# Gated output products of two branches placed between the heads of the attention, four more projections beside branch C

## The chip, the cores and the metric

The kernel runs on one core of one Trainium2 chip. The metric is the device time of one execution in microseconds (us); several executions are timed, and the median is compared. Engines are named as in the profile: PE is TensorE's matmul, PEld its weight load, DVE is VectorE, ACT is ScalarE, POOL is GpSimd, SP is SyncE, whose queue issues all the DMA transfers here. Lower is better.

## What is computed

One inference step of a backbone with two layers on 128 context tokens and 512 latent tokens (640 columns in the kernel), 1024 channels. Each layer normalises and modulates the input to `h`, projects `h` with one wide matrix, feeds three mixers (A grouped-query attention, B multi-head latent attention, C a bidirectional scan), and merges them. Cut from the reference:

```python
def _merge(gates, ya, yb, yc, lp):
    ga, gb, gc = jnp.split(jax.nn.sigmoid(gates), 3, axis=-1)
    mixed = ga * (ya @ lp['w_oa']) + gb * (yb @ lp['w_ob']) + gc * (yc @ lp['w_oc'])
    return mixed @ lp['w_out']

def _latent_mixer(h, lp, row, col, ctx_k, ctx_v, ctx_ckv, ctx_kr, s0_f, s0_b):
    a_q, a_k, a_v, a_z, b_q, b_ckv, b_kr, b_z, c_in, c_z, gates = _split_in(h @ lp['w_in'])
    q, k, v = _a_qkv(a_q, a_k, a_v, lp)
    ...
    ya = _block_attention(...) * jax.nn.silu(a_z)
    ...
    yb = _mla_attend(qb, ckv_all, kr_all, lp) * jax.nn.silu(b_z)
    yc, _, _ = _branch_c(c_in, s0_f, s0_b, lp)
    yc = yc.astype(h.dtype) * jax.nn.silu(c_z)
    return _merge(gates, ya, yb, yc, lp)
```

The products of the change are the three terms of `mixed`: each branch's output (512 channels) times its output matrix, times its sigmoid gate, summed over the branches.

## The kernel before

All of one layer's activations lie with channels on the 128 partitions and the 640 tokens along the free dimension, so that a tile is 128 x 640, worked on in two halves of 320. Each float32 matrix product is made of three matmuls on operands that are split in a high and a low part (`mm3`, L177): ScalarE casts the high part, and VectorE or GpSimd (`self.sub`) subtracts to get the low one. A weight tile is loaded from memory in one or two pieces, cast and subtracted in `load_w1` (L182).

A layer has four stages.

- **Branch C.** Four head pairs `p` go through preparation (`c_prep`, `c_pairs`, `c_inverse`: a long chain on VectorE) and a scan of ten dependent steps (`c_scan`, L700). While pair p is scanned ("period p", L1442), a generator with other work is advanced by `pump` (L201) at a rate worked out from how much it holds: the preparation of pair p+1, and `fillers`: projections of `h` that depend on nothing of the scan. A filler is one projection of 128 channels, `proj_half` twice (L218): 2 x 8 x 3 = 48 matmuls of 320 columns. `PLAN[l]['share']` says how many fillers go before the first scan and into each of the four periods. The list `early` names the projections for attention that are made here and spilled to memory (`spill`, L434, into `cmd[w]`); the 24 gate projections (`gate`, L1249, into `gsp`) follow. Numbers in `early` are projection tiles: 18 to 21 queries of A, 22 and 23 its key and value, 24 to 27 A's output gate paths, 28 to 33 queries of B, 34 to 37 its gate paths, 38 its latent. In period 3 the generator also holds `attention_start` (L1191), with `at` fillers at its six places. Here `c_out` of the pair before runs first, branch C's working memory is closed (`ctx_e.close()`), and A's keys are made by `a_keys` (L1005): `tok` (L888) projects, transposes into the tile `pqt` and copies to `kn` and `vn`.
- **Attention** (L1208). Eight head pairs, four of A and then four of B, each with two heads (`head`, L943): scores `sc` in four blocks, maximum, exponential, transposes `pp`, split, and the product with the values `po`. Between these steps `pump` advances a generator `stream(i)` by `PLAN[l]['rates'][i] / 18`: it prepares the next pair and makes the projections that are not early. `pair_out` (L982) multiplies the pair's output by its gate path and writes it to memory (`ysp`). The generator's rest is drained behind each pair. `PLAN[l]['gates']` can place gate projections here; since all 24 are made beside branch C, the list is empty when attention begins. Fillers share one PSUM bank (tag `f`, `f=1`), and `self.sub` is GpSimd in this stage.
- **Merge** (`merge`, L1258), once for each branch in the order C, A, B. It reads the branch output back (`yr` from `ysp`), splits it, and for each of four weight tiles makes two output tiles `dt`: 2 x 2 x 4 x 3 = 48 matmuls into `pm`, an eviction that multiplies by one plus the gate `gt` (read from `gsp`), and a sum over branches in the tile `mx`, which stays on chip. The last branch splits the sum into `hh` and `hl`. Eight PSUM banks are open here (`f=8`).
- **Out-projection** (`outproj`, L1289), with the next layer's normalisation behind it.

Programs for the engines aren't run in the order in which the functions are called: a planner orders the instructions of each engine by simulated time, first by this order and then by what it takes to be ready, so that later work is issued early when nothing earlier can go.

## Time and profile before

| | us |
|---|---|
| runs | 2320.34, 2323.94, 2329.52 |
| median | 2323.94 |
| profiled execution, its own time | 2325.66 |
| its span, first to last instruction | 2323.9 |
| layer 0: branch C, attention, merge, out-projection | 41 to 774, to 1047, to 1129, to 1195 |
| layer 1: the same | 1195 to 1895, to 2172, to 2254, to 2323.9 |

The stage borders are read from the first scores and the last outputs of attention and from the first matmuls of merge and out-projection; they are good to a microsecond or two, because neighbouring stages overlap. In a table by windows each engine's column is the time in which it ran something, with the number of instructions behind it; PEclk is the mean granted clock of TensorE as a share of full speed.

### The profile page before, as it was taken

The numbers are of one execution on the slowest core, as the hardware profiler recorded it, in microseconds if no ns is written. First come the engines' busy times: TensorE is split into PE (matmuls) and PEld (weight loads), VectorE is DVE, ScalarE is ACT, GpSimd is POOL, SyncE is SP. The second block draws the span as 40 slices with busy tenths as digits, with TensorE's granted clock in tenths as the row PEclk, the third lists the DMA queues.
The fourth block names the chain that finished last, engine by engine and source line by source line (L and its number), as shares of the span: only waits on it lengthen the run. The fifth ranks groups of instructions, "written<-read, shape, count | busy, mean of one in ns | idle before, by whom it ended". The sixth has DMA issues, their size and how long they took to land.

```text
span 2323.9 us, 40367 instructions
## 1 busy us (share of the span) xinstructions
PE 2130.8 (92%) x15380; PEld 2016.8 (87%) x15380; DVE 1589.3 (68%) x3062; ACT 1108.1 (48%) x2462; POOL 690.2 (30%) x761
## 2 busy tenths in 40 slices
PE   8899998999789889989989999999898889999898
PEld 6889998998789778879988999999898777888898
DVE  4676877867845676775648668668677568667673
ACT  4444443544443666662354444434443447667333
POOL 3332527335233221102033133253352332210011
PEclk9999989989899999999999999899797999999899
DMA  6232222222223311126612322222123231110562
GB/s 227 77 102 77 78 73 95 73 93 84 88 91 109 100 38 52 39 77 192 200 53 74 102 73 79 76 94 76 58 74 99 67 101 46 46 55 24 174 191 83
DMA packets 111762, 209.70 MB, mean 90 GB/s; under 512 B 14416, under 2 KB 33488, under 8 KB 111568
## 3 DMA queue, kind: packets, MB, share of 16 engines
q1 hardware_dynamic: 111568, 207.12, 28.1%
q8 instruction: 121, 1.98, 0.4%
q14 instruction: 73, 0.60, 0.1%
HBM read 163.52 MB, written 43.55 MB: 89 GB/s over the span
## 4 chain that ended last, share of the span: by engine, by line
PE 65%; DVE 18%; ACT 7%; DMA 4%; issue 4%; POOL 2%; DVEq 0%; SPq 0%; ACTq 0%; POOLq 0%
PE pcm L225 10%; PE pcm L226 10%; PE pcm L227 10%; PE sc L958 3%; PE sca L767 2%; PE pm L178 2%; PE pm L179 2%; PE pm L180 2%; DVE wlo L175 2%; PE pA L611 2%; PE pp L973 2%; PE px L679 1%; DVE nm L961 1%; PE scb L782 1%; ACT whi L174 1%
## 5 line engine op out<-in xcount | busy, mean ns | idle before, releaser
L225 PE MATMUL pcm<-hh,whi 128*128 128x320 f32 x1952 | 636.0, 326 | 21.7 <-DVE modc L252 6.7
L227 PE MATMUL pcm<-hh,wlo 128*128 128x320 f32 x1952 | 626.1, 321 | 13.7 <-DVE wlo L175 13.6
L226 PE MATMUL pcm<-hl,whi 128*128 128x320 f32 x1952 | 625.9, 321 | 0.0
L225 PEld LDWEIGHTS pcm<-hh,whi 128*128 128x128 f32 x1952 | 381.3, 195 | 29.4 <-DVE modc L252 7.9
L227 PEld LDWEIGHTS pcm<-hh,wlo 128*128 128x128 f32 x1952 | 380.2, 195 | 18.0 <-DVE wlo L175 16.9
L174 ACT CAST whi<-wraw 128x512 fp32r<-128x512 f32 (+1 forms) x356 | 226.6, 666 | 331.3 <-PE pcm L226 122.0
L226 PEld LDWEIGHTS pcm<-hl,whi 128*128 128x128 f32 x1952 | 381.5, 195 | 1.5
L175 DVE TENSOR_TENSOR wlo<-wraw,whi 128x512 fp32r<-128x512 f32 (+1 forms) x262 | 224.4, 871 | 95.1 <-ACT whi L174 91.3
L175 POOL TENSOR_TENSOR wlo<-wraw,whi 128x512 fp32r<-128x512 f32 x94 | 124.1, 1337 | 195.1 <-ACT whi L174 171.1
L778 POOL COPY ubd<-VZ 64x128 f32<-64x128 f32 x160 | 68.0, 425 | 328.1 <-ACT VZ L775 291.1
L164 DVE TENSOR_TENSOR pl<-pp,ph 128x512 fp32r<-128x512 f32 x160 | 108.4, 685 | 47.8 <-ACT ph L163 46.7
L178 PE MATMUL pm<-yh,whi 128*128 128x320 f32 x384 | 121.7, 317 | 7.1 <-DVE OT L995 3.0
L163 ACT CAST ph<-pp 128x512 fp32r<-128x512 f32 x160 | 92.4, 587 | 64.5 <-PE pp L973 53.9
L961 DVE TENSOR_REDUCE nm<-sc 128x1 f32<-128x640 f32 x128 | 104.4, 818 | 25.0 <-PE sc L958 23.6
L179 PE MATMUL pm<-yl,whi 128*128 128x320 f32 x384 | 121.3, 316 | 0.0
L180 PE MATMUL pm<-yh,wlo 128*128 128x320 f32 x384 | 121.0, 315 | 0.0
L963 ACT ACTIVATE P<-sc,nm 128x640 f32<-128x640 f32 x128 | 102.0, 798 | 18.7 <-DVE nm L961 14.4
L973 PE MATMUL pp<-small,P 128*128 128x128 f32 x640 | 102.2, 280 | 7.2 <-ACT P L963 4.3
L973 PEld LDWEIGHTS pp<-small,P 128*128 128x128 f32 x640 | 80.9, 144 | 24.9 <-ACT P L963 5.3
L611 PE MATMUL pA<-L,BK 128*128 128x128 f32 x640 | 90.7, 285 | 11.4 <-ACT AB L616 7.8
L767 PE MATMUL sca<-VZ,L 128*128 128x64 f32 x640 | 93.3, 285 | 7.7 <-DVE VZ L799 7.6
L996 POOL TENSOR_TENSOR OT<-OT,z 128x640 f32<-128x640 f32 x16 | 27.8, 1736 | 239.7 <-DVE OT L995 216.2
(375 smaller groups left out, 5021.6 us busy)
## 6 DMA issues: line engine op xcount, KB each, us to landing
wraw<-in_win SPq DMA_DIRECT2D x156, 256.0 KB, 2.9
wraw<-in_wg SPq DMA_DIRECT2D x96, 256.0 KB, 3.1
wraw<-in_wmod SPq DMA_DIRECT2D x64, 256.0 KB, 2.9
gsp<-gt SPq DMA_DIRECT2D x48, 320.0 KB, 3.1
gt<-gsp SPq DMA_DIRECT2D x48, 320.0 KB, 3.4
wraw<-in_wo SPq DMA_DIRECT2D x24, 512.0 KB, 4.4
cm<-gsl SPq DMA_DIRECT2D x26, 320.0 KB, 2.5
wraw<-in_wmod SPq DMA_DIRECT2D x16, 512.0 KB, 6.5
```

Of the source, the lines that this page charges most:

```text
L174: self.S.copy(out=hi[part], in_=raw)
L175: sub.tensor_tensor(out=lo[part], in0=raw, in1=f32(hi[part]), op=ALU.subtract)
L178: self.PE.matmul(out, lhsT=lh, rhs=rh, start=first, stop=False)
L179: self.PE.matmul(out, lhsT=lh, rhs=rl, start=False, stop=False)
L180: self.PE.matmul(out, lhsT=ll, rhs=rh, start=False, stop=last)
L225: PE.matmul(p[0:m, 0:H], lhsT=wh[:, kt], rhs=self.hh[:, kt, rs], start=(kt == 0), stop=False)
L226: PE.matmul(p[0:m, 0:H], lhsT=wh[:, kt], rhs=self.hl[:, kt, rs], start=False, stop=False)
L227: PE.matmul(p[0:m, 0:H], lhsT=wl[:, kt], rhs=self.hh[:, kt, rs], start=False, stop=(kt == KT - 1))
L611: PE.matmul(pA[:, j * 128:(j + 1) * 128], lhsT=BK[:, u].rearrange("p a s -> p (a s)"), rhs=L1[h][:, u].rearrange("p a s -> p (a s)"), star ...
L767: PE.matmul(a4[:, d, h], lhsT=L1[h][:, uu[d]].rearrange("p a s -> p (a s)"), rhs=VZ[h][:, cc[d], :], start=(h == 0 and d == 0), stop=False ...
L961: V.tensor_reduce(out=nm, in_=sc[:, :, 0:H], axis=AX.XY, op=ALU.max, negate=True)
L973: PE.transpose(p[:, qt * 128:(qt + 1) * 128], Ps[qt][:, t * 128:(t + 1) * 128], ident)
```

## The change

Four things are changed.

1. `merge` is split into `merge_y` (read back and split a branch's output, now one tile `yhl` of 128 x 2 x 4 x 640) and `merge_tile` (one weight tile, 48 matmuls, a generator that yields after every six). Attention calls them inside `stream(i)`: `merge=[0, 1, 1, 2, 0, 1, 1, 2]` tiles in the eight pairs, branch C's four during A's pairs and branch A's four during B's pairs. Only branch B's four remain in the stage behind attention.
2. The sum over branches no longer stays in `mx`: it is written to memory (`mxd`) after branch C, read and written again for branch A, and read for branch B.
3. `early` has four more entries (32, 33, 24, 35), and `share` grows by two fillers in period 2 and two in period 3 of layer 0, by one and three in layer 1. `rates` are set anew; the parameter `gates` goes.
4. To make room, A's key tile `KT` becomes two tiles, and branch B's head keys (`KH`, `KL`) reuse their two buffers.

The diff, cut to its core:

```diff
-    dict(share=[7, 5, 5, 7, 13], fb=[0, 0, 3], at=[3, 2, 1, 0, 2, 1], rate=1.0,
-         early=[38, 29, 19, 20, 21, 26, 37, 23, 28, 18, 30, 31, 34],
-         gates=[1, 0, 0, 0, 0, 1, 1, 0], rates=[8, 8, 22, 30, 21, 16, 25, 13]),
-    dict(share=[8, 6, 7, 7, 9], fb=[0, 0, 1], at=[3, 0, 2, 0, 2, 0], rate=0.8,
-         early=[26, 38, 18, 19, 30, 29, 22, 23, 28, 21, 20, 31, 34],
-         gates=[1, 0, 0, 0, 0, 0, 0, 0], rates=[5, 11, 12, 22, 31, 16, 21, 9]),
+    dict(share=[7, 5, 5, 9, 15], fb=[0, 0, 3], at=[3, 2, 1, 0, 2, 1], rate=1.0,
+         early=[38, 29, 19, 20, 21, 26, 37, 23, 28, 18, 30, 31, 34, 32, 33, 24, 35],
+         merge=[0, 1, 1, 2, 0, 1, 1, 2], rates=[8, 16, 20, 30, 16, 18, 26, 18]),
+    dict(share=[8, 6, 7, 8, 12], fb=[0, 0, 1], at=[3, 0, 2, 0, 2, 0], rate=0.8,
+         early=[26, 38, 18, 19, 30, 29, 22, 23, 28, 21, 20, 31, 34, 32, 33, 24, 35],
+         merge=[0, 1, 1, 2, 0, 1, 1, 2], rates=[8, 16, 20, 30, 16, 18, 26, 18]),
...
-        self.KT = KTt = self.kp.tile([128, 2, 2, 768], F32R, tag="KT", name="KT")
+        self.KT = KTt = [self.kp.tile([128, 2, 768], F32R, tag="KT", name="KT", bufs=2) for _ in range(2)]
...
-        KH = ap.tile([128, 768], F32R, tag="KH", name="KH", bufs=2)
-        KL = ap.tile([128, 768], F32R, tag="KL", name="KL", bufs=2)
+        KHL = self.kp.tile([128, 2, 768], F32R, tag="KT", name="KHL", bufs=2)
+        KH, KL = KHL[:, 0], KHL[:, 1]
...
+            yw = {}
+            def units(i):
+                br = 2 if i < 4 else 0
+                if br not in yw:
+                    yw[br] = self.merge_y(l, br, self.ap, "yhl", self.ap)
+                for _ in range(self.plan.merge[i]):
+                    yield from self.merge_tile(l, br, todo[br].pop(0), yw[br], wp, gp, ps)
...
                 yield from self.gate_z(es[i], l, W_AZ if i < 4 else W_BZ, wp, ps)
-                yield from units(n // 2)
                 if 3 <= i < 7:
                     self.b_pair2(l, e, ps)
                     self.b_head(l, e, 0, ps)
-                yield from units(n - n // 2 if i < 7 else len(gates))
+                yield from units(i)
                 return e
...
+    def merge_y(self, l, b, pool, tag, yp):
+        yhl = pool.tile([128, 2, 4, T], F32R, tag=tag, name="yhl", bufs=1)
         for k in range(4):
-            yr = gp.tile([128, T], F32, tag="yr", name="yr")
-            nc.sync.dma_start(out=yr, in_=self.ysp[b][k])
-            self.split(yh[k // 2][:, k % 2], yl[k // 2][:, k % 2], yr, 0.5)
+            yr = yp.tile([128, T], F32, tag="yr", name="yr", bufs=self.nyr)
+            self.nc.sync.dma_start(out=yr, in_=self.ysp[b][k])
+            self.split(yhl[:, 0, k], yhl[:, 1, k], yr, 0.5)
+        return yhl
+
+    def merge_tile(self, l, b, dp, yhl, wp, gp, ps):
+        nc, V, G = self.nc, self.V, self.G
+        oh, ol = self.load_w1(wp, self.I["wo"][l, b, dp])
+        for j in range(2):
+            dt = dp * 2 + j
+            c0 = j * 128
+            gt = gp.tile([128, T], F32, tag="gt", name="gt")
+            nc.sync.dma_start(out=gt, in_=self.gsp[b][dt])
+            if b != 2:
+                m = gp.tile([128, T], F32, tag="m", name="m", bufs=self.nm)
+                nc.sync.dma_start(out=m, in_=self.mxd[dt])
+            for half in range(2):
+                hs = slice(half * H, half * H + H)
+                pm = ps.tile([128, 512], F32, tag="f", name="pm")
+                for k in range(4):
+                    self.mm3(pm[:, 0:H], oh[:, k, c0:c0 + 128], ol[:, k, c0:c0 + 128], yhl[:, 0, k, hs],
+                             yhl[:, 1, k, hs], k == 0, k == 3)
+                    if k % 2:
+                        yield
+                V.scalar_tensor_tensor(out=gt[:, hs], in0=gt[:, hs], scalar=1.0, in1=pm[:, 0:H], op0=ALU.add, op1=ALU.mult)
+            if b != 2:
+                (G if b == 0 else V).tensor_tensor(out=gt, in0=m, in1=gt, op=ALU.add)
+            if b != 1:
+                nc.sync.dma_start(out=self.mxd[dt], in_=gt)
+            else:
+                self.split(self.hh[:, dt], self.hl[:, dt], gt, 0.5)
...
-                gp = pool(ctx, f"gp3{l}", 2)
+                self.nyr, self.nm = 2, 3
+                gp = pool(ctx, f"gp3{l}", 3)
...
-                    self.merge(l, 2, wp, gp, yp, mx, ps)
-                    self.merge(l, 0, wp, gp, yp2, mx, ps)
...
-                self.merge(l, 1, wp, gp, yp, mx, ps)
+                yhl = self.merge_y(l, 1, yp, "yhl", gp)
+                for dp in range(4):
+                    self.play(self.merge_tile(l, 1, dp, yhl, wp, gp, ps))
```

## Rows read from the trace of the kernel before

**Rows 1.** The page: busy us (share of the span) xinstructions of each engine.
```profile
PE 2130.8 (92%) x15380; PEld 2016.8 (87%) x15380; DVE 1589.3 (68%) x3062; ACT 1108.1 (48%) x2462; POOL 690.2 (30%) x761
```

**Rows 2.** Busy time by windows, five stages (columns: window and length, engines, clock, DMA).
```profile
core 0: us, PE busy (x) PEld busy (x) DVE busy (x) ACT busy (x) POOL busy (x), PEclk, DMA share, GB/s
41.00:774.00 733.00, 669.47 (x5230) 645.25 (x5228) 509.12 (x1021) 330.69 (x756) 282.01 (x321) 0.94 0.28 88
774.00:1047.00 273.00, 248.03 (x1524) 215.78 (x1525) 202.12 (x377) 181.10 (x413) 46.98 (x39) 0.95 0.16 52
1047.00:1129.00 82.00, 82.00 (x557) 82.00 (x557) 52.47 (x75) 22.15 (x26) 14.60 (x9) 0.99 0.64 196
...
1195.00:1895.00 700.00, 642.18 (x4864) 624.25 (x4863) 491.58 (x983) 302.50 (x696) 243.57 (x297) 0.92 0.25 79
1895.00:2172.00 277.00, 251.40 (x1565) 222.22 (x1566) 199.37 (x378) 184.11 (x420) 49.63 (x40) 0.95 0.17 54
```

**Rows 3.** Groups of instructions in layer 0's merge window: xcount, busy us, mean ns, idle before.
```profile
L178 PE MATMUL pm<-yh,whi 128*128 128x320 f32 x186 | 57.8, 311 | 0.0
...
L175 DVE TENSOR_TENSOR wlo<-wraw,whi 128x1024 fp32r<-128x1024 f32 x13 | 18.3, 1407 | 2.1 <-ACT whi L174 2.0
...
L1280 DVE SCALAR_TENSOR_TENSOR gt<-gt,pm 128x320 f32<-128x320 f32 x28 | 12.9, 483 | 12.8 <-DMA gt<-gsp 7.9 <-PE pm L179 2.9 <-PE pm L180 1.9
...
L1285 DVE TENSOR_TENSOR gt<-mx,gt 128x640 f32<-128x640 f32 x6 | 4.9, 821 | 0.1
...
L166 ACT ACTIVATE yh<-yr 128x640 fp32r<-128x640 f32 x6 | 4.3, 737 | 15.3 <-DMA yr<-ysp 10.2 <-PE pm L179 5.1
L167 DVE SCALAR_TENSOR_TENSOR hl<-gt,hh 128x640 fp32r<-128x640 f32 x5 | 4.1, 820 | 0.8 <-ACT hh L166 0.8
```

**Rows 4.** Timeline where layer 0's attention ends: start us, us, engine, line, tiles, idle before.
```profile
1045.22 2.01 POOL L996 TENSOR_TENSOR OT<-OT,z 128x640 f32<-128x640 f32 x1 [15.79 <-DVE OT L995]
1045.23 0.61 PE L178 MATMUL pm<-yh,whi 128*128 128x320 f32 x1 [1.49 <-DVE OT L995]
```

**Rows 5.** DMA issues of the page: xcount, KB each, median us from issue to landing.
```profile
yr<-ysp SPq DMA_DIRECT2D x24, 320.0 KB, 3.3
...
ysp<-OT SPq DMA_DIRECT2D x16, 320.0 KB, 2.3
```

**Rows 6.** Timeline of PE and of ACT around the end of period 2, layer 0.
```profile
613.93 0.38 PE L895 MATMUL pqt<-small,qcm 128*128 128x128 f32 x2
...
657.96 0.74 ACT L896 COPY kn<-pqt 128x512 f32<-128x512 f32 x2
```

**Rows 7.** Busy time by windows: ends of branch C, layer 0 and then layer 1.
```profile
612.00:655.00 43.00, 29.10 (x281) 26.85 (x279) 29.36 (x68) 14.71 (x42) 12.81 (x24) 0.68 0.19 63
...
700.00:733.00 33.00, 31.77 (x233) 30.95 (x232) 14.61 (x37) 11.67 (x32) 7.74 (x10) 0.95 0.31 99
733.00:774.00 41.00, 35.31 (x262) 33.67 (x262) 21.89 (x53) 14.87 (x32) 16.95 (x12) 0.97 0.50 154
...
1775.00:1815.00 40.00, 31.42 (x246) 28.70 (x244) 21.45 (x57) 8.66 (x29) 13.89 (x28) 0.70 0.09 31
...
1835.00:1865.00 30.00, 25.20 (x165) 23.43 (x162) 12.51 (x33) 15.53 (x39) 5.90 (x10) 0.89 0.34 108
1865.00:1895.00 30.00, 23.64 (x152) 22.26 (x151) 20.70 (x38) 9.38 (x22) 12.36 (x8) 0.89 0.30 94
```

**Rows 8.** Busy time by windows: the densest head pair of each layer's attention.
```profile
986.00:1020.00 34.00, 32.35 (x220) 29.48 (x220) 25.74 (x43) 24.71 (x57) 2.28 (x2) 1.00 0.25 82
...
2103.00:2136.00 33.00, 32.74 (x227) 30.22 (x226) 24.18 (x42) 23.21 (x53) 2.28 (x2) 1.00 0.03 11
```

**Rows 9.** Single tiles and lines: xcount, duration ns min/median/max, first and last start.
```profile
L175 POOL TENSOR_TENSOR wlo<-wraw,whi x13: 1263/1269/1296, 773.0 to 951.6; 128x512 fp32r<-128x512 f32 x13
...
L1283 POOL TENSOR_TENSOR mx<-mx,gt x16: 1562/1577/2628, 1077.4 to 2226.8; 128x640 f32<-128x640 f32 x16
...
L164 DVE TENSOR_TENSOR pl<-pp,ph x160: 671/684/693, 784.3 to 2163.2; 128x512 fp32r<-128x512 f32 x160
```

**Rows 10.** Waits of PE in layer 0's attention: us in total, times, longest us.
```profile
PE pq L1065 <- DVE z L424: 2.6, 1, 2.6
```

More of the change, by code (lines that the diff above doesn't have):

```diff
@@ L155, in __init__ @@
         self.bsp = [dr.tile([128, T], F32, tag=f"bsp{p}", name=f"bsp{p}") for p in range(4)]
+        self.mxd = [dr.tile([128, T], F32, tag=f"mxd{k}", name=f"mxd{k}") for k in range(KT)]
         self.zsp = [dr.tile([128, T], F32, tag=f"zsp{p}", name=f"zsp{p}") for p in range(4)]
@@ L1039, in a_keys @@
                     for c in range(2):
-                        S.copy(out=KTt[c * 64:c * 64 + 64, g, j, t0 * 128:(t0 + n) * 128],
+                        S.copy(out=KTt[g][c * 64:c * 64 + 64, j, t0 * 128:(t0 + n) * 128],
                                in_=p[g * 64:g * 64 + 64, 0:n * 128])
@@ L1066, in a_pair2 @@
             self.split_q(QT, slice(t0 * 128, (t0 + n) * 128), p[:, 0:n * 128])
-        e.keys = [[(QT[:, h], self.KT[:, g, 0]), (QT[:, h], self.KT[:, g, 1])] for h in range(2)]
+        e.keys = [[(QT[:, h], self.KT[g][:, 0]), (QT[:, h], self.KT[g][:, 1])] for h in range(2)]
         e.VS = lambda h: self.VSa[:, :, g, :]
@@ L1206, in attention_start, with attention @@
         return [e, (yield from self.a_pair(l, 1, wp, gp, ps))]
-    def attention(self, l, es, wp, gp, ps, gates):
+    def attention(self, l, es, wp, gp, ps):
         with self.tc.tile_pool(name=f"ap{l}", bufs=1, reuse_waits="tile") as self.ap:
-            def units(n):
-                for _ in range(min(n, len(gates))):
-                    yield from gates.pop(0)
+            yw = {}
[5 more added lines that the diff above has]
+                    yield from self.merge_tile(l, br, todo[br].pop(0), yw[br], wp, gp, ps)
             def stream(i):
-                n, e = self.plan.gates[i], None
+                e = None
                 if i < 3:
@@ L1408, in run @@
                     self.early.add((l, w))
-                ng = sum(plan.share) - len(units)
-                units += [self.gate(l, *g, wp, st, ps) for g in gates[:ng]]
-                del gates[:ng]
+                units += [self.gate(l, *g, wp, st, ps) for g in gates]
+                assert len(units) == sum(plan.share)
                 mods = [(l, ct) for ct in range(2 * KT, 3 * KT)]
@@ L1481, in run @@
                 ps = P(f"psB{l}", f=1, pt=2, po=1, S=2)
-                self.attention(l, x, wp, st, ps, [self.gate(l, *g, wp, st, ps) for g in gates])
+                self.nyr, self.nm = 1, 1
+                self.attention(l, x, wp, st, ps)
                 self.sub = self.V
@@ L1488, in run @@
                 self.pieces, self.nraw, self.nw = 1, 2, 2
-                gp = pool(ctx, f"gp3{l}", 2)
+                self.nyr, self.nm = 2, 3
+                gp = pool(ctx, f"gp3{l}", 3)
                 mp = pool(ctx, f"mx{l}", 1, side="right")
-                mx = mp.tile([128, KT, T], F32, tag="mx", name="mx")
                 wop = pool(ctx, f"wop{l}", 1, side="right")
-                yp = pool(ctx, f"yw{l}", 4)
-                with ExitStack() as ctx2:
-                    yp2 = pool(ctx2, f"yv{l}", 4)
-                    self.merge(l, 2, wp, gp, yp, mx, ps)
-                    self.merge(l, 0, wp, gp, yp2, mx, ps)
+                yp = pool(ctx, f"yw{l}", 1)
                 op = pool(ctx, f"op{l}", 2)
-                self.merge(l, 1, wp, gp, yp, mx, ps)
-                xs = mp.tile([128, KT, T], F32, tag="mx", name="xs")
+                yhl = self.merge_y(l, 1, yp, "yhl", gp)
+                for dp in range(4):
+                    self.play(self.merge_tile(l, 1, dp, yhl, wp, gp, ps))
+                xs = mp.tile([128, KT, T], F32, tag="xs", name="xs")
                 self.outproj(l, xs, wop, wp, op, ps)
```

26 lines of the change are left out of this document (1 added, 25 removed).

## The prediction

> **What bounds the kernel now.** I read the page first: TensorE (PE) is called busy 92% of the span, VectorE (DVE) 68% [rows 1]. So TensorE's issue looks like the bound, and the question is where it still has holes. The stage table [rows 2] answers it. Each layer has four stages: branch C (733.0 and 700.0 us), attention (273.0 and 277.0), the gated output products, here "merge" (82.0; layer 1's is alike and stands for it), and the out-projection. The column to read is PEld, the weight loads, one ahead of each matmul: 100% of the merge window, 88% and 89% of the two branch C windows, 79% and 80% of the attentions. The merge issued 557 matmuls in 82.00 us, 0.147 us each; this is the price of a dense matmul here. A "unit" (a projection tile or a merge tile) is 48 matmuls, 7.07 us. The merge has 12 units a layer and no hole; attention has 57.2 and 54.8 us without a weight load, branch C 87.8 and 75.8. The change carries units from the full stage into the two that have holes.
>
> The Trainium skill, Trace Analysis, Identifying the Most-Contended Engine, calls matmul busy share a bad metric and names weight-load share instead. The trace agrees: in the merge matmuls overlap so far that means of 311 ns [rows 3] pass at 0.147 us each. Read by matmul busy, attention would have 25.0 and 25.6 us of room for 28.3 us of work; with half of it usable attention would cost 31 us and not the 14 below, and the sum would be 2282.
>
> **The change part by part.**
>
> Merge. Eight of the 12 units a layer leave (branches C and A), four stay (branch B). Before, TensorE ran merge matmuls without a hole from 1045.23 [rows 4] to the end of the merge window at 1129, 84 us. After, 192 matmuls are 28.3 us, but branch B needs the last head pair's output, which has just been made. That chain was hidden under branches C and A: GpSimd's product 2.0 us [rows 4], write 2.3, read back 3.3 [rows 5], cast 0.74 and subtraction 0.82 [rows 3], 9.2 us. Its cover now is the first three of four k steps of eight PSUM banks, 72 matmuls or 10.6 us, just enough. Behind it VectorE is late next: 16 evictions of 0.483, 8 additions of 0.82, 8 subtractions of 0.82, and weight subtractions of 1.41 for two more output tiles and the first two out-projection tiles [rows 3], 7.7 + 6.6 + 6.6 + 5.6 = 26.5 us. I take 9.2 + 26.5 = 36 us, so the stage gives back 48 a layer, 96 in all. Bounds: TensorE alone, 28.3 (gain 56); transfers alone, about 9.6 MB (gates and partial sums 5.2, weights 2.1 and 1.0, outputs 1.3) at the 196 GB/s of the window [rows 2], 49 us (gain 35). I stay nearer to VectorE's figure because its instructions are all in the rows, while 196 GB/s is what was asked for, not a limit.
>
> Branch C. Four more projections a layer: two in period 2 and two in period 3 of layer 0, one and three in layer 1. Each also issues two weight loads and one write-out on SyncE's queue, which is mostly idle there; their casts, subtractions and evictions go to ScalarE and VectorE, 45% and 69% busy in that stage [rows 2]. Period 2 ends in a hole. The transposes of a projected tile (pqt) were issued at 613.93, long before their turn, and their copies out to kn ran only at 657.96 [rows 6]: the memory of kn is that of branch C, free only when the normalised scan output of pair 2 is out. Until then the transposes hold the PSUM banks of the projections and no projection runs. In 612 to 655 weight loads ran 26.85 of 43.00 us at a granted clock of 0.68, a mix of the levels 1.2 and 2.4 GHz; in layer 1, 1775 to 1815, 28.70 of 40.00 at 0.70 [rows 7]. Units that come earlier in the order push later ones into the hole: 14.1 us into 16.2, 7.1 into 11.3. I put them at nothing. If the cover is gone they cost 21.2; if the clock stays at the lower level there, two units want twice 14.1 and don't fit. Period 3's units have less: 14.1 us against 2.1 + 7.3 of room in layer 0, 21.2 against 6.6 + 7.7 in layer 1 [rows 7]. I let half of the room be usable: 14.1 - 4.7 = 9.4 and 21.2 - 7.2 = 14.0, so branch C costs 23 in both layers. Ends: all room usable, 12; none anywhere, 57.
>
> Attention. Four projections leave (28.3 us), eight merge tiles come (56.6), net 28.3 a layer. Weight loads and added pitch make 215.8 + 28.3 = 244.1 and 250.5 us. The densest pairs before had 29.48 of 34.00 (87%) and 30.22 of 33.00 (92%) [rows 8]. At 87% the stages take 281 and 288, at 92% 265 and 272. I take 87%, nearer to a stage in which most pairs have work, less 1.8 a layer for a dozen branch C matmuls that already ran inside the last pair: +6 and +9, about 14 with the rounding. Ends: -8 a layer, and +28.3 with nothing hidden. The other engines have room: VectorE is at 74%, ScalarE 66%, GpSimd 17% [rows 2]. Per layer GpSimd gains 8 weight subtractions net of 1.27 and 8 additions of 1.58 [rows 9], 22.8 us on an engine with 226 idle; VectorE gains 32 evictions of 0.483 and 8 subtractions of 0.82, 22 us on 71 idle, less what four projections took. SyncE's queue gets 64 transfers (16 weight loads, 16 gates, 24 of partial sums, 8 branch outputs) and four read-backs for eight weight loads that go; the stage moves 52 GB/s against 196 in the merge, so I put them at nothing too. The split key buffer (KT in two halves that later hold branch B's keys) adds a wait of b_head on branch A's scores; these run early in a pair, and I put it at nothing; the first branch B keys late by one pair's scores would be a few us once a layer.
>
> Sum: -96 + 23 + 14 = -59. The profiled execution took 2325.66 us, 1.7 over the median of 2323.94 and inside the runs shown; 59 off the median is 2265.
>
> **The rivals.**
>
> Better: the holes take nearly all. Branch C costs 12, attention gains 8 a layer: 2324 - 96 + 12 - 16 = 2224. For it: the merge shows that TensorE can be at 100%. Against: no attention pair was above 92%.
>
> Late merge tiles: the planner leaves the last two tiles of branch A in pair 7 to the drain behind the heads, where nothing hides them: 14.1 a layer, 2293. For it: tile sums of pairs 0 and 4 are empty and pair 7 has two. Against: the planner ran merge matmuls inside pair 7 before.
>
> Slower, no room: each moved unit costs its 7.07 us in the new place, 113 in all, against 96: 2341. This is the case that the change only shifts work; it decides when less than 15% of the moved work (17 of 113) falls into holes. Against it: the holes of [rows 7].
>
> Slower, one bank: in attention fillers share one PSUM bank. A projection hands it over twice, a merge tile four times: 16 handovers a layer before, 8 + 32 = 40 after. One handover shows as a TensorE wait: 2.6 us for z's eviction [rows 10]. If each of the 24 new ones stalled so, 62 a layer would replace attention's 14: 2265 - 14 + 123 = 2374. It turns the change into a loss above (59 + 14) / 48 = 1.5 us each. Against: one of about 16 handovers shows so.
>
> GpSimd against VectorE: if GpSimd's added 22.8 us a layer blocked VectorE and VectorE bound, 46 us would go: 2311. Against: GpSimd's subtraction in attention took 1263 to 1296 ns and VectorE's 671 to 693 over all 160 [rows 9], no stretch; its additions reached 2628 at most. The Trainium skill, SBUF — State Buffer, SBUF: two separate sides, describes such a rule: one of the two holds a shared port pair for its whole instruction while the other waits. By it this rival would come true.
>
> **How the numbers follow.** Forecast 0.62 (2265, by the bounds some 2240 to 2300), better 0.13, late tiles 0.10, port 0.05, no room 0.06, one bank 0.04. The range 2228 to 2314 leaves out the two slower cases and half of the better one, under 0.2. About 0.5%, 12 us, is what a measurement can tell from no change. Faster: 0.62 less a tail of 0.03, plus 0.13 and 0.10, is 0.82; within 0.5%: 0.05 and the tail, 0.08; slower 0.10.
>
> **What the profile of the changed kernel would show.** The merge window from the last attention matmul to the first out-projection one: 36 us (28 to 48) with VectorE near full in it, else my chain is wrong. Attention 273 and 277 become about 279 and 286 with weight loads at 87%. Branch C grows by about 9 and 14, the holes at the ends of period 2 get shorter by two units and one, and their granted clock rises from 0.68 and 0.70. If attention grows by more than 28, with waits of TensorE for evictions of pm, the one-bank rival is right; a stretched GpSimd or VectorE row says the port; a tail of pm matmuls behind the last PV product of pair 7 says late tiles. The prediction is wrong if the holes don't shrink, or if the first merge matmul of branch B comes more than 10 us after the last of attention.

## The result, and the profile after

The changed kernel took 2395.84 us (median of four runs, 2393.60 to 2397.68), the kernel before 2322.52 (four runs): 1.031 times, 95% interval 1.0286 to 1.0334. It is slower by 73 us where 59 less were forecast. Its profiled execution took 2393.60 us with a span of 2391.8, 67.9 more than that of before. Line numbers of the changed kernel are higher by one to some fifteen.

The page's busy times, as in [rows 1]: TensorE has the same 15380 matmuls, and smaller shares of a longer span.

```profile
PE 2149.5 (90%) x15380; PEld 2034.3 (85%) x15380; DVE 1577.8 (66%) x3062; ACT 1112.1 (46%) x2478; POOL 703.0 (29%) x777
```

The stages by windows, attention and merge of layer 0, then of layer 1; they answer to [rows 2].

```profile
core 0: us, PE busy (x) PEld busy (x) DVE busy (x) ACT busy (x) POOL busy (x), PEclk, DMA share, GB/s
805.00:1117.00 312.00, 269.59 (x1647) 239.17 (x1646) 209.66 (x397) 180.88 (x409) 63.90 (x52) 0.92 0.25 80
1117.00:1173.00 56.00, 40.64 (x237) 39.18 (x238) 23.65 (x35) 13.34 (x16) 4.70 (x4) 0.79 0.65 224
1946.00:2265.00 319.00, 274.37 (x1679) 243.58 (x1679) 211.10 (x408) 185.98 (x420) 66.13 (x54) 0.92 0.26 85
2265.00:2322.00 57.00, 43.21 (x265) 41.64 (x266) 25.04 (x39) 13.56 (x16) 6.43 (x5) 0.88 0.67 225
```

Layer 1's attention of the kernel before begins with its first scores at 1892, 3 us ahead of the border in [rows 2], and ends at 2171. Cut like the rows above it is

```profile
1892.00:2171.00 279.00, 252.44 (x1576) 223.00 (x1576) 201.77 (x385) 184.14 (x420) 50.60 (x41) 0.95 0.18 55
```

Read the second column of busy times, PEld, against the length. The attentions had 57.2 and 56.0 us without a weight load; they have 72.8 and 75.4 now. They were given 28.3 us of work each, grew by 39 and 40, and their holes grew. The merge stage was one block at 100%; 30% and 27% of it are empty now, at a granted clock of 0.79 and 0.88.

For the comparison of kernels I cut every trace at four events of a layer: branch C begins with the first `plo` matmul and ends with the first context scores (`scc`), attention ends with the last product of `OT` and `z` on GpSimd, merge with the first `pout` matmul. Layer 0 / layer 1:

| kernel | its us | before beside it | branch C | attention | merge |
|---|---|---|---|---|---|
| before | 2323 | | 733 / 696 | 273 / 279 | 82 / 83 |
| changed | 2396 | 2323 | 763 / 710 | 312 / 319 | 56 / 57 |
| e1 projections only | 2340 | 2326 | 763 / 714 | 255 / 263 | 83 / 81 |
| e2 branch C's tiles only | 2367 | 2326 | 760 / 706 | 297 / 306 | 60 / 60 |
| e3 other bank | 2334 | 2326 | 762 / 706 | 314 / 320 | 29 / 28 |
| e5 last pair free | 2369 | 2326 | 762 / 705 | 312 / 336 | 42 / 36 |
| e6 bank alone | 2360 | 2320 | 733 / 696 | 291 / 300 | 81 / 82 |
| e7 merges alone, bank | 2324 | 2320 | 729 / 695 | 328 / 340 | 28 / 29 |
| e8 C's tiles in B's pairs | 2364 | 2320 | 738 / 697 | 311 / 323 | 61 / 58 |
| e9 third gate buffer | 2377 | 2320 | 765 / 706 | 306 / 317 | 51 / 57 |
| e10 merges alone | 2406 | 2330 | 734 / 694 | 342 / 350 | 53 / 57 |
| e11 bank in pairs 4 to 6 | 2358 | 2330 | 765 / 709 | 322 / 329 | 27 / 28 |
| e12 merges alone, the same | 2343 | 2330 | 737 / 699 | 331 / 337 | 29 / 35 |
| e13 spread tiles | 2343 | 2330 | 767 / 707 | 310 / 329 | 27 / 28 |
| e14 period 2's units alone | 2324 | 2317 | 741 / 707 | 266 / 265 | 83 / 83 |
| e15 merges, period 2, bank | 2351 | 2317 | 746 / 702 | 329 / 339 | 27 / 29 |
| e16 the same, spread | 2373 | 2317 | 738 / 702 | 340 / 362 | 29 / 28 |
| e17 with gate buffer | 2352 | 2317 | 735 / 702 | 330 / 353 | 29 / 29 |
| e18 merges, bank, buffer | 2326 | 2321 | 733 / 692 | 331 / 337 | 28 / 28 |
| e19 change, bank, buffer | 2330 | 2321 | 762 / 707 | 314 / 320 | 28 / 27 |

e1 to e17 are single executions beside one of before; in the last comparison 19 executions of before lay between 2314.50 and 2336.64, so a difference of less than some 15 us between single times says little, and the stages say more. Changed less before by stage: branch C +30.6 and +13.3, attention +39.2 and +39.9, merge -25.7 and -26.6, out-projection -2.9 and +0.1: 67.9, all of the difference.

Two places of layer 0 stand for the loss. First the tail. The timeline behind the heads, and a wait of SyncE's queue in it:

```profile
1120.82 0.49 DVE L1295 SCALAR_TENSOR_TENSOR gt<-gt,pm 128x320 f32<-128x320 f32 x1 [3.84 <-DMA gt<-gsp]
1132.11 0.49 DVE L1295 SCALAR_TENSOR_TENSOR gt<-gt,pm 128x320 f32<-128x320 f32 x1 [3.66 <-PE pm L181]
1134.29 0.32 SPq L1299 DMA_DIRECT2D mxd<-gt  x1
1136.44 0.80 SPq L1271 DMA_DIRECT2D yr<-ysp  x2
1137.29 0.42 SPq L174 DMA_DIRECT2D wraw<-in_wo  x1
1142.79 1.04 ACT L175 CAST whi<-wraw 128x1024 fp32r<-128x1024 f32 x1 [1.88 <-DMA wraw<-in_wo]
1143.89 0.64 PE L179 MATMUL pm<-yhl,whi 128*128 128x320 f32 x1 [11.82 <-ACT whi L175]
```

```profile
SPq L1271 <- DMA mxd<-gt: 1.8, 1, 1.8
```

The heads end at 1117, but branch A's last tile still runs, a bank at a time, until its last partial sum goes out at 1134.29. Only when that write has landed are branch B's output, weights and gates asked for (1136.44, 1137.29), and TensorE stands idle for 11.82 us. In the kernel before, the read-backs for the merge began at 1026.62, during pair 7; the first were branch C's, which had long been there. Then the first merge matmuls of branch B run slowly. Windows of that stretch:

```profile
1131.00:1144.00 13.00, 1.18 (x6) 0.78 (x4) 2.26 (x4) 2.52 (x3) 1.53 (x1) 0.50 0.55 193
1144.00:1150.00 6.00, 6.00 (x33) 6.00 (x34) 2.71 (x3) 1.90 (x3) 0.00 (x0) 0.77 1.04 410
1156.00:1173.00 17.00, 17.00 (x118) 17.00 (x117) 14.77 (x23) 8.15 (x10) 0.00 (x0) 1.00 0.73 241
```

Matmul by matmul that is 6.00 us / 33 = 0.18 us at a clock of 0.77, between the levels of 1.2 and 2.4 GHz, against 17.00 / 118 = 0.144 at 1.00.

Second, a border of pairs. TensorE where pair 4 gives over to pair 5:

```profile
992.92 0.63 PE L1151 MATMUL pqr<-small,qr 128*64 128x128 f32 x4 [0.41 <-DVE gt L1295]
994.14 0.44 PE L921 MATMUL scc<-KHL,QT 128*128 128x128 f32 x2 [0.60 <-DVE QT L168]
998.58 0.33 PE L921 MATMUL scc<-KB,QR 96*128 96x128 f32 x1 [2.61 <-DVE QR L1158]
1002.15 0.40 PE L1151 MATMUL pqr<-small,qr 128*64 128x128 f32 x1 [2.38 <-DVE QR L1158]
```

The next pair's query transposes (`pqr`) got the f bank at 992.92, released by the eviction (`gt`) of a merge tile. Pair 5's scores had begun at 994.14 with the part that needs `KHL` and `QT` alone; the rest waited for `QR`, which is made from `pqr`. The bank is not all of this wait. ScalarE, which takes `pqr` out, first cast a projection's weights and a row of a branch output for the merge tiles (`yhl`), and came to `QR` at 996.10:

```profile
994.02 1.14 ACT L175 CAST whi<-wraw 128x512 fp32r<-128x512 f32 x2
995.06 0.73 ACT L167 ACTIVATE yhl<-yr 128x640 fp32r<-128x640 f32 x1
996.10 0.59 ACT L1156 ACTIVATE QR<-pqr 32x512 fp32r<-32x512 f32 x1
```

Pair 4 has no merge tile by plan. The ones that ran there are the two of pair 3, a pair late, in both layers. The merge matmuls alone, in changed's pair 4 and then in pair 3 of e3, the kernel with these transposes in another bank (below), where they ran in time:

```profile
950.00:999.00 49.00, 15.81 (x96) 14.26 (x96) 3.90 (x8) 0.91 0.30 99
913.00:971.00 58.00, 15.84 (x96) 14.21 (x96) 4.38 (x9) 0.93 0.38 121
```

PE's waits in layer 0's attention, in us, times, longest; neither `scc` nor `pqr` had more than 0.9 from QR in the kernel before:

```profile
PE sc L959 <- ACT P L964: 6.4, 7, 2.0
PE scc L921 <- DVE QR L1158: 4.6, 2, 2.6
PE pqr L1151 <- DVE QR L1158: 2.6, 2, 2.4
PE pqr L1151 <- DVE z L425: 1.9, 1, 1.9
PE pm L179 <- DVE gt L1295: 1.6, 3, 0.8
```

### The profile page after: what moved, and what is told of

Read it like the earlier page. It is cut to its first block, busy times and chain, and to the rows that moved or that the text cites. A ratio compares the mean times of both kernels' runs of the same rounds, so it can differ in the third digit from the quotient of the medians.

```text
span 2391.8 us, 40580 instructions
## 1 busy us (share of the span) xinstructions
PE 2149.5 (90%) x15380; PEld 2034.3 (85%) x15380; DVE 1577.8 (66%) x3062; ACT 1112.1 (46%) x2478; POOL 703.0 (29%) x777
## 4 chain that ended last, share of the span: by engine, by line
PE 35%; DVE 8%; ACT 4%; DMA 3%; issue 2%; POOL 1%; DVEq 0%; SPq 0%; ACTq 0%; POOLq 0%
PE pcm L226 5%; PE pcm L227 5%; PE pcm L228 5%; PE pm L179 2%; PE pm L180 2%; PE pm L181 2%; PE pout L179 1%; PE sc L959 1%; PE pout L181 1%; PE pout L180 1%; PE sca L768 1%; PE pA L612 1%; PE pp L974 1%; DVE L L550 1%; DVE BK L548 1%
## 5 line engine op out<-in xcount | busy, mean ns | idle before, releaser
L176 DVE TENSOR_TENSOR wlo<-wraw,whi 128x512 fp32r<-128x512 f32 (+1 forms) x262 | 201.9, 790 | 97.4 <-ACT whi L175 94.1
L176 POOL TENSOR_TENSOR wlo<-wraw,whi 128x512 fp32r<-128x512 f32 x110 | 145.5, 1337 | 263.2 <-ACT whi L175 232.2
L179 PE MATMUL pm<-yhl,whi 128*128 128x320 f32 x384 | 125.8, 331 | 36.1 <-ACT whi L175 22.4
L964 ACT ACTIVATE P<-sc,nm 128x640 f32<-128x640 f32 x128 | 102.0, 798 | 41.8 <-DVE nm L962 36.0
L180 PE MATMUL pm<-yhl,whi 128*128 128x320 f32 x384 | 121.2, 317 | 0.0
L181 PE MATMUL pm<-yhl,wlo 128*128 128x320 f32 x384 | 118.4, 316 | 0.0
L962 DVE TENSOR_REDUCE nm<-sc 128x1 f32<-128x640 f32 x128 | 104.3, 819 | 20.5 <-PE sc L959 19.4
L179 PEld LDWEIGHTS pm<-yhl,whi 128*128 128x128 f32 x384 | 74.8, 195 | 41.0 <-ACT whi L175 23.0
L768 PEld LDWEIGHTS sca<-VZ,L 128*128 128x128 f32 x640 | 91.7, 211 | 18.5 <-DVE VZ L800 17.7
```

The costliest lines, as they stand in the source:

```text
L176: sub.tensor_tensor(out=lo[part], in0=raw, in1=f32(hi[part]), op=ALU.subtract)
L179: self.PE.matmul(out, lhsT=lh, rhs=rh, start=first, stop=False)
L180: self.PE.matmul(out, lhsT=lh, rhs=rl, start=False, stop=False)
L181: self.PE.matmul(out, lhsT=ll, rhs=rh, start=False, stop=last)
L768: PE.matmul(a4[:, d, h], lhsT=L1[h][:, uu[d]].rearrange("p a s -> p (a s)"), rhs=VZ[h][:, cc[d], :], start=(h == 0 and d == 0), stop=False ...
L962: V.tensor_reduce(out=nm, in_=sc[:, :, 0:H], axis=AX.XY, op=ALU.max, negate=True)
```

## The experiments

None of the kernels leaves out a part of the computation. "Changed" is the changed kernel.

**The two parts apart.** The kernel before with the projections only, then with the merge tiles only:

```diff
 # e1, on before
-    dict(share=[7, 5, 5, 7, 13], ... early=[..., 31, 34],
+    dict(share=[7, 5, 5, 9, 15], ... early=[..., 31, 34, 32, 33, 24, 35],
 # e10, on changed
-    dict(share=[7, 5, 5, 9, 15], ... early=[..., 31, 34, 32, 33, 24, 35], ... rates=[8, 16, 20, 30, 16, 18, 26, 18]
+    dict(share=[7, 5, 5, 7, 13], ... early=[..., 31, 34], ... rates=[8, 16, 20, 36, 16, 26, 26, 18]
```

> The kernel before with the four more early projections and their shares alone; all merge tiles stay behind attention. Attention loses 4 projections (28.3 us of matmuls) a layer, the merge stage stays. Theory 1 (the loss sits between branch B's heads and in the tail, branch C costs what the changed kernel shows, 31 + 13): branch C grows by about 44 in both layers, attention gives back 10 to 25 a layer, so 2322 + 44 - 35 = about 2331, between 2315 and 2350. Theory 2 (a unit costs its 7.07 us wherever it stands): 2322, no change. Theory 3 (the four projections are the main cause, attention had room for them): 2355 or more.

> The changed kernel with before's projections beside branch C (no four early ones); banks and merge tiles as changed. Theory 1 (the two parts of the change add): the changed kernel less what the projections alone cost, 2392 - 14 = 2378 (2365 to 2390), branch C as in before. Theory 2 (the loss comes from the two parts together, branch C's growth shifting the attention): within 12 of before, 2311 to 2335.

e1: branch C +30.5 and +17.6, attention -17.9 and -15.8. Moving 28.3 us a layer cost more in branch C than attention gave back; 14 us slower, inside the range of its theory 1. e10 took 2406, 76 above its before, and misses both its theories; the parts don't add (14 + 76 is more than 73): with the merge tiles in it, attention gains more from losing four projections (342 to 312, 350 to 319) than it did without them (273 to 255, 279 to 263).

> The kernel before with only period 2's early projections (two in layer 0, one in layer 1); period 3's four and the merge tiles stay as before. Theory 1 (period 2's units run in its hole and cost nothing, and attention loses 0.6 to 1.0 of their 7.07 us): branch C as before within 4 a layer, attention -9 to -14 in layer 0 and -4 to -7 in layer 1, 2302 to 2313 beside a before of 2326. Theory 2 (each unit costs its 7.07 us and a stall in branch C as period 3's did): branch C +14 to +25 and +7 to +12, 2326 to 2345.

e14 is e1 with `share=[7, 5, 5, 9, 13]` and `[8, 6, 7, 8, 9]`, so only period 2's. Branch C +8.4 and +10.2, attention -7.3 and -14.6; the time, 7 above its before, is within what single executions tell, and the 13 to 24 us less of its theory 1 didn't come. The units were not free, and attention gave back about what branch C took.

**The bank.** The next pair's transposes and values off the f bank, in changed (e3) and in the kernel before (e6); e11 does it in pairs 4 to 6 alone, e12 the same without the early projections:

```diff
-            p = ps.tile([128, 512], F32, tag="f", name="pqr")
+            p = ps.tile([128, 512], F32, tag=self.prep, name="pqr")
 # the same for pvb, and (e3, e6, e7, e8, e18, e19) for pq
 # self.prep is "pt" in attention; in e11 and e12 only from pair 4 on, in e15 to e17 from pair 3 on
```

> The changed kernel, but the next pair's query transposes and value products (pq, pqr, pvb) take the two PSUM banks of the head's transposes (tag pt) in attention and no longer the one bank that merge tiles use. Theory 1 (merge tiles hold the one bank, the next pair's preparation comes late, its scores start cold): pairs 4 to 6 fall by 20 us a layer or more from 141, the kernel to about 2350. Theory 2 (no bank matters, the work is just too much): 2396 within 10, or slower by what the heads' transposes lose.

> The kernel before, with one edit: in attention the next pair's transposes (pq, pqr) and value products (pvb) take the two pt banks and no longer the one f bank; no merge tile moves. Theory 1 (the bank matters only where merge tiles hold it long): the time of before, 2326, within 6. Theory 2 (the one f bank already limited attention before the change): each attention falls by some 8 to 10 us, 2306 to 2310.

> The changed kernel with the next pair's transposes and value products (pqr, pvb) on the pt banks only while pairs 4 to 6 run; pairs 0 to 3 keep the f bank. Theory 1 (the bank edit costs in pairs 0 to 3, +17 to +22 a layer where it stood alone, and gains in pairs 4 to 7 and the tail): pairs 0 to 3 as in the changed kernel (146, 149), pairs 4 to 7 near 150, merge 28, 2295 to 2310. Theory 2 (the gain needs the tiles to end early in pair 3, which only the wide edit does): pairs 4 to 7 stay at 160 or more, merge above 45, 2340 to 2385.

> As the run before it, with before's projections beside branch C. Theory 1: branch C as in before, attention about 15 to 20 a layer longer than there, 2285 to 2305. Theory 2 (attention has no room for four more units): attention above 330, 2325 or more.

e3 took 2334, 62 less than changed. But the gain isn't in attention's length (314 and 320): it is the merge stage, 29 and 28 against 56 and 57. The tiles were no longer held up, none was left behind the heads, and branch B's tiles began in time. Its theory 1 named the bank, but looked for the gain in pairs 4 to 6, which fell by 14 and 7 us and not by 20 a layer. Attention by windows, both layers of e3 and then of e6:

```profile
803.00:1117.00 314.00, 280.82 (x1706) 247.97 (x1707) 214.68 (x406) 183.72 (x413) 70.24 (x55) 0.93 0.32 103
1915.00:2235.00 320.00, 286.29 (x1759) 253.51 (x1759) 218.15 (x417) 188.44 (x424) 73.05 (x57) 0.94 0.33 109
774.00:1064.00 290.00, 257.38 (x1528) 222.08 (x1529) 203.88 (x377) 181.19 (x412) 45.43 (x39) 0.93 0.15 49
1906.00:2206.00 300.00, 264.69 (x1575) 229.08 (x1575) 201.61 (x385) 184.39 (x420) 48.82 (x41) 0.93 0.16 51
```

e3's holes are 66.0 and 66.5 us where changed had 72.8 and 75.4, with the late tiles inside. Cut by pairs, at the last product of `OT` and `z`, e3's pairs 4 to 7 are 20.5 and 18.2 us shorter than changed's, its pairs 0 to 3 are 21.6 and 19.1 longer; 14.1 us of that are the two tiles that came back from pair 4. e6, the same edit without tiles, cost 40 us against its before, nearly all of it in attention (+17.5 and +21.2); both theories miss. All of that lies in pairs 0 to 3 (+16.8 and +21.6; pairs 4 to 7 +0.7 and -0.3), and its holes are 67.9 and 70.9. Why A's pairs pay so much for it stays open. e11 has the tail of its theory 1 (27 and 28) and the long B pairs of its theory 2 (178 and 180). e12 with 2343 and attentions of 331 and 337 is its theory 2: no room for four more units.

**Merge tiles elsewhere.** e2 has branch C's tiles between heads and branch A's behind attention, e5 no tile in the last pair, e8 branch C's in B's pairs and branch A's behind attention, with before's projections and the other bank, e13 is e11 with one tile in each A pair:

```diff
-merge=[0, 1, 1, 2, 0, 1, 1, 2]
+merge=[0, 1, 1, 2, 0, 0, 0, 0]   # e2
+merge=[1, 1, 1, 1, 0, 2, 2, 0]   # e5
+merge=[0, 0, 0, 0, 1, 1, 1, 1]   # e8, branch C's
+merge=[1, 1, 1, 1, 0, 1, 1, 2]   # e13
```

> The changed kernel, but branch A's four merge tiles stand behind attention again, ahead of branch B's; branch C's stay between the heads of A's pairs. Theory 1 (branch A's tiles in branch B's pairs and the tail behind them cost more than they save): pairs 4 to 7 come back to 130 us a layer or less from 167 and 169, the wait of 11.8 us ahead of branch B's first matmul goes, the merge stage is 28 us of matmuls longer, and the kernel takes about 2396 - 2 x 37 - 2 x 20 + 2 x 28 = 2338, between 2310 and 2355. Theory 2 (a unit costs 7.07 us anywhere): four units out of attention and four into the merge cancel, 2396 within 10.

> The changed kernel with merge tiles at other places: branch C's one in each of pairs 0 to 3, branch A's two in pairs 5 and 6, none in pair 7. Tail part of theory 1 (branch B's loads can't start before the last branch A tile has freed its memory, and pair 7's tiles run behind the heads): branch B's loads start before attention ends, the 11.8 us wait goes, and the stretch from the last head output to the out-projection falls from 56 to about 40 a layer; attention itself stays within 10 us: about 2396 - 32 = 2364, between 2345 and 2385. Theory 2: the same units, 2396 within 10.

> Before's projections, the next pair's transposes and values on the pt banks, and only branch C's four merge tiles between heads, one in each of the pairs 4 to 7; branch A's tiles stand behind attention with branch B's. Theory 1 (a merge tile costs its 7.07 us of TensorE wherever it stands): merge gives back 28 a layer, attention takes 28 a layer, 2326 within 8. Theory 2 (the pairs of branch B have holes that one tile each can fill, and the loss of the changed kernel came from crowding two into one pair): attention +15 a layer, 2300 (2290 to 2312).

> The changed kernel with the narrow bank edit of pairs 4 to 6 and branch C's tiles one to each of the pairs 0 to 3 (two stood in pair 3). Theory 1 (two tiles in pair 3 lag into pair 4): pairs 4 and 5 shorter by 5 to 10 a layer than with the tiles as changed, 10 to 20 us less in all. Theory 2 (a tile costs 7 us wherever it stands): within 6 of the kernel with the narrow edit alone.

e2 against e1: four tiles (28.3 us) made attention 41.8 and 42.9 longer and merge only 23 and 21 shorter. So branch C's tiles alone lose, before any tail; e2 has changed's rates and buffers too, so it is not the tiles by themselves. e5's stages behind the heads are 42 and 36: the tail falls by 14 and 21, but layer 1's attention takes 16 back. e8 was worse than either theory. e13 is 14 below e11, as its theory 1 had it, but inside what single executions tell; e16 further on is 23 above e15 by the same move (rates set along with it in both). No rule came of where the tiles stand.

**The gate rows.** A buffer more for `gt` in attention (e9):

```diff
-            gt = gp.tile([128, T], F32, tag="gt", name="gt")
+            gt = (self.ap if j and self.nm == 1 else gp).tile([128, T], F32, tag="yr" if j and self.nm == 1 else "gt", name="gt", bufs=1 if j and self.nm == 1 else None)
```

> The changed kernel with a third buffer for the gate rows of the merge tiles in attention (the second row tile of each merge tile takes a buffer of its own), all else as changed. Theory 1 (the single bank and TensorE's full order set the pace of the merge tiles): the changed kernel's 2392 within 8. Theory 2 (the evictions of pm wait for gate rows, which wait for the write-out of the row tile before, and so hold the bank): pairs 3 to 7 and the tail lose 10 to 15 a layer, 2362 to 2372, and the wait of the last evictions for gt is gone.

In attention (`nm` is 1) the second row tile of each merge tile takes a buffer of its own. e9 took 2377, between its theories. VectorE's waits in changed from 1105 to 1135, and then in e9 from 1080 to 1135:

```profile
DVE gt L1295 <- PE pm L181: 11.9, 6, 3.7
DVE gt L1295 <- DMA gt<-gsp: 6.0, 2, 3.8
```

```profile
DVE gt L1295 <- PE pm L181: 10.2, 9, 2.1
DVE yhl L168 <- ACT yhl L167: 6.2, 2, 6.0
DVE gt L1295 <- DMA gt<-gsp: 2.4, 1, 2.4
```

The wait for gate rows fell from 6.0 to 2.4 us, and merge is still 51 and 57: layer 0 gained some 5 us of its 28, layer 1 none. Most of the tail is made by the late tiles and not by the gates.

**Merge tiles, bank and buffer.** e7 is e10 with e3's edit and higher rates; e18 is e7 with e9's buffer, e19 puts both edits on changed. e15 keeps e11's edit from pair 3 on and period 2's projections, e16 spreads branch C's tiles as e13 does, e17 adds the buffer.

> The changed kernel with before's projections beside branch C (no four early ones, so attention keeps them) and the next pair's transposes and values on the pt banks. Theory 1 (effects add): the changed kernel with that bank (2333.5) less what the projections alone cost (2340.2 - 2325.8 = 14.3): 2319, 2305 to 2335; branch C as in before (732, 696), attention about 273 + 57 = 330 and 336, merge 28. Theory 2 (TensorE has no room left in attention, units there cost more than 7.07 us each, as branch C's tiles did with 10.6): attention beyond 345, time above 2345.

> Merge tiles as changed, next pair's transposes and values of branch B on the pt banks from pair 3 on, and of the early projections only period 2's. Theory 1 (attention pays every unit in full, so each one that branch C hides is a gain): the 2322 of the merges alone with the other bank, less 10 to 14 and 5 to 7, 2300 to 2308; less up to 16 more, as the A pairs keep their bank for pq. Theory 2 (the holes of the head pairs grow with what is left out, as in the projections alone): 2318 to 2330.

> The run before it with branch C's tiles one to each of the pairs 0 to 3. Theory 1 (two tiles in pair 3 crowd its end): 10 to 20 us less than that run, as with the narrow bank edit (2357.7 to 2343.5). Theory 2 (once the bank is free it doesn't matter where the tiles stand): within 6 of it.

> The run before it with the third gate buffer. Theory 1 (gate rows hold the f bank in part): 5 to 15 us less, as in the changed kernel (2392 to 2377). Theory 2 (the gate buffer matters only where everything queues on one bank): within 5.

> The merge tiles alone with the other bank (2322 beside a before of 2320), with the third gate buffer added. Theory 1 (gate rows still hold the merge tiles' bank at times): 15 to 20 us less, as in the changed kernel (2392 to 2377) and with spread tiles (2373 to 2352): 2302 to 2308, faster than before. Theory 2 (attention pays every unit in full and its holes are those of the kernel before, 60 and 64 us against 59 and 58, so there is nothing left for a buffer to give): 2317 to 2326, no change.

> The changed kernel with the other bank (2333.5) and the third gate buffer. Theory 1: 15 to 20 us less, 2313 to 2319. Theory 2: within 6 of 2333.

e18 took 2326.13 (ten runs) beside 2320.86 (19): ratio 1.0018, 0.9994 to 1.0042, no change. e19: 1.0032, 1.0010 to 1.0054. No kernel tried beat the one before. e15 to e17, with fewer units in attention than e7, came out 26 to 49 us above it; e15 and e16 miss both their theories. Fewer units are not their only difference: they leave the f bank to `pq` and to pairs 0 to 2, and e12, which has e7's plan and a like edit, was 19 above e7 already (8 if each is taken against its own before). e17 is 21 below e16, more than the 15 of its theory 1; but e7 and e18 differ by nothing that can be told, nor do e3 and e19, so the buffer gives nothing once the whole edit has freed the bank. e18 by windows, attention and merge of layer 0, then of layer 1:

```profile
774.00:1104.00 330.00, 302.40 (x1895) 270.91 (x1895) 219.90 (x411) 192.87 (x432) 79.19 (x64) 0.95 0.32 104
1104.00:1132.00 28.00, 28.00 (x186) 28.00 (x186) 20.42 (x30) 10.24 (x12) 0.38 (x1) 0.97 0.62 207
1887.00:2224.00 337.00, 305.56 (x1950) 275.50 (x1950) 227.02 (x420) 195.77 (x440) 83.15 (x65) 0.97 0.32 107
2224.00:2252.00 28.00, 28.00 (x188) 27.92 (x187) 19.77 (x30) 10.02 (x13) 0.36 (x1) 0.97 0.59 195
```

This is the cleanest form of the change's main idea. The merge stage is 28 us of full weight loads, less than the forecast 36. Attention holds eight more tiles: its weight loads grew by 55.1 and 52.5 us, its length by 57 and 58. The holes are 59.1 and 61.5 us, where the kernel before had 57.2 and 56.0, so against that kernel the added tiles filled none. The merge stages gave back 110 us, the attentions took 116. Against e6, which has the bank edit and no tiles, they cost only 39.9 and 37.0 us of their 56.6, so one could think that they do run in holes, and that the edit's own cost hides it. e12 speaks against that: it leaves A's pairs, where that edit costs, on the f bank, and its attentions are still 58.1 and 57.4 us longer than before, with holes of the same size, 56.3 and 56.6 us:

```profile
778.00:1109.00 331.00, 303.11 (x1896) 274.73 (x1895) 219.23 (x410) 193.15 (x432) 80.69 (x63) 0.93 0.31 104
1900.00:2237.00 337.00, 306.93 (x1941) 280.39 (x1941) 220.51 (x419) 194.53 (x438) 83.35 (x65) 0.94 0.30 96
```

The merge matmuls alone, behind the last product of the heads in changed (1117 and 2265), and in the last pair of e18 in layer 0:

```profile
1117.00:1133.00 16.00, 11.53 (x48) 10.06 (x48) 1.96 (x4) 0.68 0.51 171
2265.00:2283.00 18.00, 12.14 (x72) 10.57 (x72) 3.04 (x7) 1.00 0.51 164
```

```profile
1084.00:1104.00 20.00, 2.00 (x7) 1.84 (x8) 0.00 (x0) 0.84 0.33 106
```

One tile (48 matmuls) and one and a half (72) of branch A were late in changed. In e18 the only merge matmuls of the last pair are branch B's first ones, and none of branch A's is left.

## Why the prediction was wrong

**Attention: the step that failed first.** I took the share of the densest pair before (87%, [rows 8]) as what the whole stage could reach and got +6 and +9 (15 together, where I wrote 14). The stage reached 76.7% (239.17 of 312) and 76.4%, less than its 79% and 80% before [rows 2], and 82% in e18. The holes were real, but time without a weight load isn't room: eight tiles more left 56 to 61 us of it in e12 and e18, where the kernel before had 57.2 and 56.0. I take it to lie where a pair waits for its own chain, from exponential to transposes, split and value product (of PE's waits above, that of `sc` for the exponential is the largest); this place is argued and not shown. The other reading, room by matmul busy, gave 31, nearer but still far: the attention term is 79. e3 has 81 without the late tiles and with fewer stalls, so the term doesn't hang on those. Its two halves can be priced. Eight tiles a layer cost 58.1 and 57.4 (e12) or 57.4 and 58.2 (e18), their full 56.6 and a little more. The four projections that left gave back 17.9 and 15.8 (e1), not the 28.3 that I took off for them. Together that is 116 - 34 = 82. In changed 2.5 tiles (17.7 us) ran behind the border, and holes that grew by 15.6 and 19.4 us stood in their place.

**One bank: a rival with the right place and a wrong price.** I gave it 0.04 and counted handovers of `pm`, 2.6 us each [rows 10]. PE's waits of `pm` for `gt` are 1.6 us in layer 0's attention and 4.1 behind it. The price came through the other users of that bank: merge tiles ran a pair late and at last behind the heads, the next pair's `pqr` queued behind them, and scores waited for `QR`. In e10 that row stands at 9.0 us:

```profile
PE scc L921 <- DVE QR L1158: 9.0, 4, 3.4
```

That the bank is in the chain is shown by e3, 62 us less than changed by that edit alone. e7 is 82 below e10, but has higher rates too. Rates alone don't bring the tiles in time: in e12, with e7's rates and the f bank up to pair 3, pair 3's two tiles still ran in pair 4. What the crowded bank costs in attention by itself isn't shown, since e6 has a cost of its own.

**Merge.** The forecast was 36 a layer, the result 56 and 57, e18's 28. The chain of 9.2 us [rows 3 to 5] is covered, as I wrote: in e18 the weight loads fill the stage. VectorE's 26.5 behind it does not come: with 20 of 28 us busy it is not the limit, and TensorE's 28.3, my lower bound, was the value. In changed, the rival of late merge tiles came on top, with 1 and 1.5 tiles where I had two; but I priced it at their 14.1 us, and it cost 28 and 29 a layer (56 and 57 against e18's 28), because branch B's loads waited behind them. The condition I had written for being wrong, a first matmul of branch B over 10 us late, is the row at 1143.89.

**Branch C.** 44 where I forecast 23, inside the ends of 12 and 57. Period 3's units cost 21.7 and 17.7 us from the copy to `kn` on, where I had 9.4 and 14.0. In layer 0 that is more than the 14.1 of the two units, so no room was used and something was lost besides; in layer 1 it is 3.5 less than the 21.2 of the three. Period 2's were to cost nothing. The copy to `kn` [rows 6] came, counted from the start of branch C, 8.9 us later in layer 0 and 4.5 earlier in layer 1; with these units alone (e14) 5.3 and 10.7 later. The windows of the two holes, answering to [rows 7]:

```profile
621.00:664.00 43.00, 39.14 (x375) 36.97 (x373) 28.23 (x68) 18.66 (x48) 11.93 (x23) 0.88 0.29 95
...
1806.00:1846.00 40.00, 31.60 (x268) 29.40 (x267) 19.88 (x46) 12.34 (x31) 10.68 (x20) 0.58 0.21 69
```

Layer 0's hole took 10.1 of the 14.1 us and its clock rose from 0.68 to 0.88, as I wrote, yet its end moved; layer 1's stayed empty, and its clock went from 0.70 to 0.58.

**No room, the mechanism I gave 0.06.** 113 against 96, 2341: e18 comes nearest to that case with the stalls taken out: 116 against 110, and so no change, since its merge stages gave back more than my 96. Add to 2341 the tail, 28 a layer more than e18's, and one has 2397 for a measured 2395.84. That agreement is chance, as the pieces differ (branch C less than 57, attention more). What the runs do show is this: forecast and result are 131 us apart, and e3's one edit, which frees the bank and ends the tail, takes back 62. In e3 the rest is attention (81 where I had 14) and branch C (38 where I had 23), less a merge stage that gave back 109 and not 96.

**The port.** The operations that I had looked at hardly stretch. GpSimd's subtraction, its addition and VectorE's subtraction, answering to [rows 9], and two rows of the end of branch C:

```profile
L176 POOL TENSOR_TENSOR wlo<-wraw,whi x21: 1259/1273/1851, 804.0 to 1108.2; 128x512 fp32r<-128x512 f32 x21
L1297 POOL TENSOR_TENSOR gt<-m,gt x16: 1529/1570/1583, 1053.3 to 2281.0; 128x640 f32<-128x640 f32 x16
L165 DVE TENSOR_TENSOR pl<-pp,ph x160: 672/692/694, 818.1 to 2249.6; 128x512 fp32r<-128x512 f32 x160
L868 DVE TENSOR_TENSOR rp<-kn,ropeA x8: 209/214/1312, 675.0 to 677.1; 128x64 f32<-128x64 f32 x8
L862 POOL TENSOR_TENSOR rp<-kn,ropeA x1: 1309/1309/1309, 675.2 to 675.2; 128x512 f32<-128x512 f32 x1
```

Medians of 1273, 1570 and 692 ns stand against 1269, 1577 and 684, with GpSimd at 63.90 us in the stage instead of 46.98. The port rule of the Trainium skill, SBUF — State Buffer, SBUF: two separate sides, is not seen in the first three rows, but the last two look like it: one of eight VectorE products took 1312 ns where the others took some 214, while GpSimd ran a product of 1309 ns on the same tiles. My subtraction `pl` reads one of its operands from PSUM and could not settle the rival. The sum of such stretches can: what VectorE's operations in the two attentions took beyond the median of their kind (counting those over it by 0.1 us or more) is 14.7 us in the kernel before, 8.5 in changed and 22 in e18, far from the 46 of the rival.

**What stays open.** Why the bank edit costs 17 and 22 us in A's pairs; how much of e15 to e17's loss against e7 is the narrower bank edit; and why the same spreading of tiles gave -14 once and +23 once. The planner's order is in all of these, as every edit reshuffles it; no run held that order fixed. The split key buffer was not run alone, but e18 has it, with holes only 1.9 and 5.5 us larger than before.

## What to carry to other kernels

Time without a weight load need not be room: before moving work from a stage that is full into one that looks 80% full, price it at its full length there and let the trace argue it down, not up. Ask which buffers and banks the moved work shares with the chain that sets the stage's pace, since its loss comes by those. And look at what starts when the last moved piece ends: one to one and a half tiles, 7 to 11 us of matmuls, held back loads and cost 28.

## What the runs showed of the hardware

Gaps cost more than their length. While the last tile of layer 0 ran with waits between its parts, the mean granted clock was 0.68 (1117 to 1133); it was 0.50 in the window of TensorE's 11.82 us wait and 0.77 in the 6 us behind it, so that the merge matmuls restarted at 0.18 us each, against 0.144 at 1.00. In attention the mean granted clock went with the stalls, too: 0.92 and 0.92 in changed, 0.95 and 0.97 in e18, which has more matmuls. One VectorE operation of 0.21 us took 1.31 beside a GpSimd operation of the same length on the same tiles.
